# Another order of issue at the seams of a two-layer hybrid decoder trunk in float32 on one core

## The chip, the cores and the metric

The kernel runs on one core of a Trainium2 chip. The metric is the device time of one execution in microseconds, as the median of several runs; the profile is of one execution, whose own time stands below. Engines are named as the trace does: PE is TensorE's matmul, PEld its weight load, DVE VectorE, ACT ScalarE, POOL GpSimd, SP SyncE. Each engine works through its own queue in the order in which the program issues its instructions, and waits at the first one whose operands or buffers are not ready.

## The reference

Two layers work on x of shape 1 x 512 x 1024 in float32. Each layer is this:

```python
h  = rmsnorm(x, ln_mix_g)
qa, ka, va, qb, kb, vb, cq, ckv, kr = split(h @ w_in)   # 3 x 512, 512, 512, 512, 768, 256, 32
ya = dilated_attention(qa, ka, va)        # 8 heads of 64, T5 bias
yb = diff_attention(qb, kb, vb, lambda)   # 4 heads; lambda from lambda_q1, k1, q2, k2
yc = latent_attention(rmsnorm(cq) @ w_uq, rmsnorm(ckv) @ w_ukv, rope(kr))   # 8 heads
m  = sum over branches of sigmoid(h @ w_gate) * (y @ w_br)
x  = x + m @ w_o
f  = rmsnorm(x, ln_ffn_g)
x  = x + (silu(f @ w_ffn_gate) * (f @ w_ffn_up)) @ w_ffn_down   # hidden 2816
```

After the second layer, the output is rmsnorm(x, final_norm_g).

## The kernel before

**Products.** Every float32 product is made of three matmuls in the faster float32 format: high part by high part, high by low, low by high. Weights arrive through SP's queue as tiles of 128 x 1024, a unit. `_hi` makes the high part with a cast on ACT, `_lo` the low part with a subtraction on DVE. `ahead(i, most)` (L272) loads units as far as the present look (`NEAR`, `FAR`, `LEAN`) allows and issues at most so many casts and splits beyond unit i; `prep(n)` makes the first n units at once. A pool of 36 wide tiles (`w`) holds weights, their parts and most intermediates.

**Jobs.** `t_job` (L295) makes a feature-major tile in one PSUM bank with 24 matmuls. `n_job` (L345) makes token-major products: four token blocks of 128 rows, a bank each, with the weights as moving operand; a unit holds two k-blocks. Its list `groups` says how many k-blocks are done for a token block before the next one has its turn. There are four PSUM banks for jobs (`d`, taken round in a ring) and four for attention (`a`).

**A layer.** The norm and its transposes come first, then the value projection. `weave` (L392) interleaves the attention's threads with the dense jobs (queries and keys, `cq`, `ckv`, the up-projections, gates, branches); it decides by a model of its own of when each engine is free, so its order is fixed when the kernel is built. Then come two `n_job`s of w_o, the FFN, and two `n_job`s of w_ffn_down, each of half the columns. All engines' instructions are recorded at L158, the helper that issues them; places are told apart by tiles.

**The start of layer 0.** `after(tb)` transposes a token block of the normed h and splits it; `prep` stands between these calls. `small_setup` is a thread of the weave that computes lambda (small dots on DVE of loaded lambda vectors) and scales of the gates.

**The FFN.** The first two groups are computed by 16 plain products in `ffn_head`, the rest by seven products per group (`P1` to `P7`, Strassen-like, with sums made before on DVE and results evicted by `evac`). The 2816 hidden columns lie in tiles of 1024 columns (`ff32`), each split into high and low by `ffsplit`. The SiLUs of the head's results come after its last product:

```python
o = K.wide(F32)
nc.scalar.activation(o[:, :512], d["X"], AF.Silu)
nc.scalar.activation(o[:, 512:], d["Y"], AF.Silu)
```

**The end.** `final_evac` (L1326 and on) adds the residual, sums squares on ACT, and after the second half calls `norm_block`, which scales both halves on DVE, with the norm's weight, and sends them out through SP.

Of the kernel before, what the change touches and what calls it, by code (L numbers as in the profile page):

```python
# [18 lines left out]
P = 128  # L19
# [148 lines left out]
class Kernel:  # L168
# [176 lines left out]
    def n_job(self, wname, layer, ks, cols, lhs, evac, groups=None, ready=None):  # L345

        w = len(cols)
        per = 1024 // w
        assert per == 2 or len(ks) % 2 == 0
        per = 2  # L350
        units = [[(wname, layer, k, cols) for k in ks[i:i + per]] for i in range(0, len(ks), per)]
        groups = groups or [1] * len(ks)

        def body(j):
            ps = None
            k0 = 0
            for g in groups:
                for tb in range(NT):
                    if g > 1 or tb == 0:
                        self.ahead(j.base + (k0 + g - 1) // per, 2)  # L360
                    if k0 == 0:
                        if ps is None:
                            ps = [None] * NT
                        ps[tb] = self.bank()
                    for kb in range(k0, k0 + g):
                        u, c = j.base + kb // per, slice(kb % per * w, kb % per * w + w)
                        h, l = self.hi[u][:, c], self.lo[u][:, c]
                        ah, al = lhs(kb, tb)
                        o = ps[tb][:, :w]
                        mm = self.nc.tensor.matmul  # L370
                        mm(o, ah, h, start=kb == 0, stop=False)
                        mm(o, ah, l, start=False, stop=False)
                        mm(o, al, h, start=False, stop=kb == len(ks) - 1)
                        if g > 1 and kb == k0 + g // 2 - 1:
                            yield
                    if k0 + g == len(ks):
                        evac(tb, ps[tb])
                    if g > 1 or tb == 1:
                        yield
                k0 += g  # L380
                for u in range((k0 - g) // per, k0 // per):
                    self.done(j.base + u)
                if g == 1:
                    yield

        return self.add_job(units, body, ready)

# [238 lines left out]
def layer(K, l, plan, state, strip, C):  # L626
# [554 lines left out]
    def ffn_head():  # L1181

        for th in range(2):
            for g in range(HEAD):
                d = G[g]
                if th == 0:
                    d["X"], d["Y"] = K.bank(), K.abank()
                for ch in range(2):
                    for kh in range(2):
                        product(d["YX"[ch]][:, th * 256:th * 256 + 256], "A%d%d" % (th + 1, kh + 1),  # L1190
                                d["B%d%d" % (kh + 1, ch + 1)], kh == 0)
                        yield
        for g in range(HEAD):
            d = G.pop(g)
            if g % 2 == 0:
                o = K.wide(F32)
                nc.scalar.activation(o[:, :512], d["X"], AF.Silu)
                nc.scalar.activation(o[:, 512:], d["Y"], AF.Silu)
                V["fg", g // 2] = o
            else:  # L1200
                f = V.pop(("fg", g // 2))
                sub(f[:, :512], f[:, :512], d["X"], ALU.mult)
                sub(f[:, 512:], f[:, 512:], d["Y"], ALU.mult)
                V["ff32"][g // 2] = f
        del SF["A21"]

    def prep(job, g, st):
# [60 lines left out]
    def ffn_run(job):  # L1268
# [6 lines left out]
        for i, (g, p) in enumerate(slots):  # L1275
# [20 lines left out]
                    before()  # L1296
                before = lambda g=g, p=p: evac(g, p)
            K.load_ahead(job.base + 2 * min(NG, slots[min(len(slots) - 1, i + 12)][0] or 4))
            if g == NG - 1 or i > len(slots) - 12:
                K.ahead(job.base + 2 * NG - 1, 1)  # L1300
                if V["nsplit"] < 3:
                    ffsplit(V["nsplit"])
            yield i
        before()
        SF.clear()
# [21 lines left out]
    def final_evac(hf):  # L1327
        def evac(tb, ps):
            t = state["x"][tb][hf]
            nc.vector.tensor_tensor(t, ps, t, op=ALU.add)  # L1330
            if hf == 0:
                state["ss"][tb] = K.small(2)
            K.sumsq(t, state["ss"][tb][:, hf:hf + 1], D)
            if hf == 1:
                xn = K.norm_block(state["x"][tb], state["ss"][tb], state["g"])
                for i in range(2):
                    nc.sync.dma_start(ap["out"][tb * P:tb * P + P, i * 512:i * 512 + 512], xn[i])
        return evac


# [75 lines left out]
                nc.sync.dma_start(state["x"][tb][hf], src[tb * P:tb * P + P, hf * 512:hf * 512 + 512])  # L1416

    def small_setup():
        yield when((), lambda: C["small_tiles"])
        C["setup_small"]()  # L1420

    j_wo = [K.n_job("w_o", l, range(KD), rng(0, 512), mblk, residual_evac(0, ffn_after)),
# [2 lines left out]
    last = l == DEPTH - 1  # L1425
    ev = final_evac if last else (lambda hf: residual_evac(hf, after))
    j_dn = [K.n_job("w_ffn_down", l, range(NF), rng(0, 512), ffblk, ev(0)),
            K.n_job("w_ffn_down", l, range(NF), rng(512, 512), ffblk, ev(1), groups=[1] * 14 + [8])]


    def drain(jobs):
# [3 lines left out]
    def run():  # L1435
        if l == 0:
# [2 lines left out]
            bias = C["setup_bias"]()  # L1439
            next(bias)  # L1440
            norm1_stats(0)
            after(0)
            next(bias)
            K.prep(1)
            norm1_stats(1)
            K.prep(3)
            norm1_stats(2)
            K.prep(4)
            next(va)
            after(1)  # L1450
            norm1_stats(3)
# [48 lines left out]
        K.look = LEAN  # L1500
        drain(j_dn[:1])
        for i, _ in enumerate(K.dense(j_dn[1:])):
            if i == 26:
                K.look = FAR

    plan.append(run)
# [35 lines left out]
```

## Time and profile before

| | us |
|---|---|
| median of 3 runs (1862.61 to 1864.9) | 1864.62 |
| the profiled execution | 1862.47 |
| its span | 1860.7 |
| PE busy in it (98%) | 1818.6 |
| DVE busy (60%) | 1111.1 |
| ACT busy (47%) | 880.3 |

The mean granted clock over the span is 0.998 of TensorE's full speed. Busy time of an engine counts from an instruction's start to its end; matmuls overlap, so one row's mean duration is longer than the distance between two starts.

### The profile page before, as it was taken

How to read it: one execution, taken by the hardware profiler on the slowest of the kernel's cores; microseconds unless marked ns; L12 is line 12 of the kernel's file. 1: busy time of each engine (PE TensorE's matmuls, PEld its weight loads, DVE VectorE, ACT ScalarE, POOL GpSimd, SP SyncE). 2: the span in 40 equal slices, each digit the busy share in tenths (PEclk: the TensorE clock that was granted, in tenths of full speed). 3: DMA queues.
4: the chain of work that ended last, by engine and by line, in shares of the span. 5: the costliest groups of instructions: out<-in, count | busy, mean ns of one | idle time of the engine just before them, and what ended most of it. 6: DMA issues, size and time to landing. Idle time of an engine off the chain costs nothing.

```text
span 1860.7 us, 27128 instructions
## 1 busy us (share of the span) xinstructions
PE 1818.6 (98%) x10588; PEld 1620.2 (87%) x10588; DVE 1111.1 (60%) x1828; ACT 880.3 (47%) x1697; POOL 251.0 (13%) x437
## 2 busy tenths in 40 slices
PE   7999999999999999999999999999999999999998
PEld 5899888888889999988889998888888889999886
DVE  4556555556455888872355565555663578788531
ACT  4456555554334545452235655555443345545430
POOL 3323422212000000000003243122110000000000
PEclk9999999999999999999999999999999999999999
DMA  7332123223340332342433221232242313233331
GB/s 267 108 96 72 52 69 97 85 80 115 124 146 23 99 106 92 113 137 69 147 121 102 69 65 47 72 102 85 69 176 79 114 54 106 91 114 103 125 102 46
DMA packets 63279, 183.14 MB, mean 98 GB/s; under 512 B 9296, under 2 KB 10768, under 8 KB 63152
## 3 DMA queue, kind: packets, MB, share of 16 engines
q1 hardware_dynamic: 58032, 173.89, 28.3%
q0 software_dynamic: 3824, 4.91, 0.9%
q10 hardware_dynamic: 1296, 2.62, 0.4%
q8 instruction: 83, 1.36, 0.3%
q14 instruction: 44, 0.36, 0.1%
HBM read 177.15 MB, written 8.16 MB: 100 GB/s over the span
## 4 chain that ended last, share of the span: by engine, by line
PE 87%; ACT 4%; DVE 4%; issue 2%; POOL 2%; DMA 1%; POOLq 0%; DVEq 0%; ACTq 0%
PE d L158 68%; PE a L158 19%; DVE w L158 3%; ACT w L158 3%; POOL s L158 1%; POOL w L158 1%; DMA w<-in_lambda_k 0%; ACT s L158 0%; DMA s<-in_c_onehot 0%; DVE s L158 0%; ACT junk L158 0%; ACT L158 0%; POOL m L158 0%; DVE f_A L158 0%; DVE f_S L158 0%
## 5 line engine op out<-in xcount | busy, mean ns | idle before, releaser
L158 PE MATMUL d<-w,w 128*128 128x512 f32 (+2 forms) x3888 | 749.4, 347 | 12.2 <-DVE w L158 6.7
L158 PEld LDWEIGHTS d<-w,w 128*128 128x128 f32 x3888 | 631.2, 190 | 96.2 <-ACT s L158 7.2
L158 DVE TENSOR_TENSOR w<-w,w 128x1024 fp32r<-128x1024 f32 (+6 forms) x594 | 597.9, 1031 | 194.8 <-ACT w L158 167.5
L158 PE MATMUL d<-h,w 128*128 128x512 f32 x1920 | 462.1, 393 | 2.8 <-DVE w L158 2.8
L158 ACT CAST w<-w 128x1024 fp32r<-128x1024 f32 (+3 forms) x454 | 399.8, 921 | 101.9 <-DVE w L158 51.7
L158 PEld LDWEIGHTS d<-h,w 128*128 128x128 f32 x1920 | 356.8, 188 | 74.5 <-DVE w L158 3.2
L158 PE MATMUL d<-w,h 128*128 128x512 f32 (+2 forms) x960 | 197.9, 355 | 11.2 <-DVE w L158 9.6
L158 PEld LDWEIGHTS d<-w,h 128*128 128x128 f32 x960 | 164.6, 189 | 30.7 <-issue 9.4
L158 ACT ACTIVATE w<-w,m 128x128 f32<-128x128 f32 x192 | 107.0, 558 | 120.8 <-DVE m L158 119.1
L158 POOL TENSOR_SCALAR m<-m 128x1 f32<-128x1 f32 (+1 forms) x44 | 15.9, 360 | 1085.9 <-ACT junk L158 1085.4
L158 PE MATMUL a<-w,w 128*128 128x256 f32 (+7 forms) x912 | 158.3, 311 | 0.0
L158 PEld LDWEIGHTS a<-w,w 128*128 128x128 f32 (+1 forms) x912 | 138.8, 190 | 11.8
L158 PE MATMUL a<-f_A,w 128*128 128x256 f32 x1104 | 147.9, 285 | 0.0
L158 PEld LDWEIGHTS a<-f_A,w 128*128 128x128 f32 x1104 | 139.6, 193 | 0.0
L158 POOL TENSOR_SCALAR w<-w,m 128x128 f32<-128x128 f32 (+3 forms) x160 | 92.6, 597 | 328.0 <-DVE m L158 219.3
L158 DVE TENSOR_TENSOR w<-a,w 128x512 fp32r<-128x512 f32 (+2 forms) x162 | 90.8, 594 | 75.7 <-ACT w L158 75.4
L158 ACT CAST w<-a 128x512 fp32r<-128x512 f32 (+2 forms) x146 | 70.9, 535 | 68.6 <-PE a L158 67.6
L158 ACT ACTIVATE junk<-s 128x512 f32<-128x512 f32 (+1 forms) x40 | 23.6, 590 | 161.4 <-DVE s L158 161.0
L158 ACT COPY s<-d 128x256 f32<-128x256 f32 (+2 forms) x104 | 39.8, 391 | 108.0 <-PE d L158 107.3
L158 POOL TENSOR_SCALAR w<-w 64x512 fp32r<-64x512 f32 (+1 forms) x96 | 69.4, 730 | 137.3 <-issue 90.1
L158 DVE TENSOR_TENSOR s<-d,s 128x512 f32<-128x512 f32 x32 | 21.9, 689 | 107.6 <-PE d L158 107.6
L158 PE MATMUL a<-ident,w 128*128 128x128 f32 x616 | 83.9, 275 | 0.1
(76 smaller groups left out, 1213.6 us busy)
## 6 DMA issues: line engine op xcount, KB each, us to landing
w<-in_weights SPq DMA_DIRECT2D x246, 512.0 KB, 3.6
w<-in_weights SPq DMA_DIRECT2D x50, 256.0 KB, 2.6
w<-in_weights SPq DMA_DIRECT2D x28, 384.0 KB, 4.4
s<-u_rep SPq DMA_DIRECT2D x24, 256.0 KB, 4.0
w<-in_weights SPq DMA_DIRECT2D x8, 288.0 KB, 2.9
w<-in_x SPq DMA_DIRECT2D x8, 256.0 KB, 7.2
s<-in_x SPq DMA_DIRECT2D x8, 256.0 KB, 5.9
x_dram<-s ACTq DMA_DIRECT2D x8, 256.0 KB, 3.6
```

Source lines behind the costliest of these rows:

```text
L158: return f(*args, **kw)
```

## The change

It puts the same computation in another order in six places. (1) `n_job` does both k-blocks of a unit, six matmuls, for a token block before it goes on to the next, where it did three; `ahead` is called for each token block, with one cast and one split, where it was called once with two; the second down job's list changes in the same way, with its look switched one yield later. (2) In `ffn_head`, the SiLU of each half is issued as soon as the half is complete, and the two products of DVE behind the head. (3) `ffn_run` spreads the three `ffsplit`s and calls of `ahead` over the last eight products, where it had called them from twelve products before the end. (4) `final_evac` multiplies by the norm's weight before the scale is known, scales one half on DVE and the other on ACT, and sends the halves out from two queues. (5) `small_setup` waits until the second `ckvT` tile is there. (6) The first unit is prepared before the first token block's transposes and splits, and the others are one apart. Layer 1 has no part in (5) and (6).

```diff
--- before.py
+++ after.py
@@ -349,15 +349,14 @@
         assert per == 2 or len(ks) % 2 == 0
         per = 2
         units = [[(wname, layer, k, cols) for k in ks[i:i + per]] for i in range(0, len(ks), per)]
-        groups = groups or [1] * len(ks)
+        groups = groups or [2] * (len(ks) // 2)
 
         def body(j):
             ps = None
             k0 = 0
             for g in groups:
                 for tb in range(NT):
-                    if g > 1 or tb == 0:
-                        self.ahead(j.base + (k0 + g - 1) // per, 2)
+                    self.ahead(j.base + (k0 + g - 1) // per, 2 if g > 2 else 1)
                     if k0 == 0:
                         if ps is None:
                             ps = [None] * NT
@@ -371,17 +370,14 @@
                         mm(o, ah, h, start=kb == 0, stop=False)
                         mm(o, ah, l, start=False, stop=False)
                         mm(o, al, h, start=False, stop=kb == len(ks) - 1)
-                        if g > 1 and kb == k0 + g // 2 - 1:
+                        if g > 2 and kb == k0 + g // 2 - 1:
                             yield
                     if k0 + g == len(ks):
                         evac(tb, ps[tb])
-                    if g > 1 or tb == 1:
-                        yield
+                    yield
                 k0 += g
                 for u in range((k0 - g) // per, k0 // per):
                     self.done(j.base + u)
-                if g == 1:
-                    yield
 
         return self.add_job(units, body, ready)
 
@@ -1189,19 +1185,20 @@
                     for kh in range(2):
                         product(d["YX"[ch]][:, th * 256:th * 256 + 256], "A%d%d" % (th + 1, kh + 1),
                                 d["B%d%d" % (kh + 1, ch + 1)], kh == 0)
+                        if th == 1 and g % 2 and kh == 1:
+                            u, n = G[g - 1]["YX"[ch]], 512 - 512 * ch
+                            if ch == 0:
+                                f = K.wide(F32)
+                            nc.scalar.activation(f[:, n:n + 512], u, AF.Silu)
+                            if ch == 1:
+                                V["ff32"][g // 2] = f
                         yield
+        for g in range(1, HEAD, 2):
+            f = V["ff32"][g // 2]
+            sub(f[:, 512:], f[:, 512:], G[g]["Y"], ALU.mult)
+            sub(f[:, :512], f[:, :512], G[g]["X"], ALU.mult)
         for g in range(HEAD):
-            d = G.pop(g)
-            if g % 2 == 0:
-                o = K.wide(F32)
-                nc.scalar.activation(o[:, :512], d["X"], AF.Silu)
-                nc.scalar.activation(o[:, 512:], d["Y"], AF.Silu)
-                V["fg", g // 2] = o
-            else:
-                f = V.pop(("fg", g // 2))
-                sub(f[:, :512], f[:, :512], d["X"], ALU.mult)
-                sub(f[:, 512:], f[:, 512:], d["Y"], ALU.mult)
-                V["ff32"][g // 2] = f
+            del G[g]
         del SF["A21"]
 
     def prep(job, g, st):
@@ -1296,10 +1293,11 @@
                     before()
                 before = lambda g=g, p=p: evac(g, p)
             K.load_ahead(job.base + 2 * min(NG, slots[min(len(slots) - 1, i + 12)][0] or 4))
-            if g == NG - 1 or i > len(slots) - 12:
+            rest = len(slots) - i
+            if rest in (8, 5, 3, 1):
+                ffsplit(V["nsplit"])
+            if rest in (6, 4, 2):
                 K.ahead(job.base + 2 * NG - 1, 1)
-                if V["nsplit"] < 3:
-                    ffsplit(V["nsplit"])
             yield i
         before()
         SF.clear()
@@ -1331,10 +1329,14 @@
             if hf == 0:
                 state["ss"][tb] = K.small(2)
             K.sumsq(t, state["ss"][tb][:, hf:hf + 1], D)
+            sub(t, t, state["g"][hf], ALU.mult)
             if hf == 1:
-                xn = K.norm_block(state["x"][tb], state["ss"][tb], state["g"])
-                for i in range(2):
-                    nc.sync.dma_start(ap["out"][tb * P:tb * P + P, i * 512:i * 512 + 512], xn[i])
+                r = K.rstd([state["ss"][tb][:, 0:1], state["ss"][tb][:, 1:2]])
+                x = state["x"][tb]
+                nc.vector.tensor_scalar(x[0], x[0], r, None, op0=ALU.mult)
+                nc.scalar.activation(x[1], x[1], AF.Copy, scale=r)
+                for i, eng in enumerate((nc.sync, nc.scalar)):
+                    eng.dma_start(ap["out"][tb * P:tb * P + P, i * 512:i * 512 + 512], x[i])
         return evac
 
 
@@ -1416,7 +1418,7 @@
                 nc.sync.dma_start(state["x"][tb][hf], src[tb * P:tb * P + P, hf * 512:hf * 512 + 512])
 
     def small_setup():
-        yield when((), lambda: C["small_tiles"])
+        yield when((("ckvT", 1),), lambda: C["small_tiles"])
         C["setup_small"]()
 
     j_wo = [K.n_job("w_o", l, range(KD), rng(0, 512), mblk, residual_evac(0, ffn_after)),
@@ -1425,7 +1427,7 @@
     last = l == DEPTH - 1
     ev = final_evac if last else (lambda hf: residual_evac(hf, after))
     j_dn = [K.n_job("w_ffn_down", l, range(NF), rng(0, 512), ffblk, ev(0)),
-            K.n_job("w_ffn_down", l, range(NF), rng(512, 512), ffblk, ev(1), groups=[1] * 14 + [8])]
+            K.n_job("w_ffn_down", l, range(NF), rng(512, 512), ffblk, ev(1), groups=[2] * 7 + [8])]
 
 
     def drain(jobs):
@@ -1439,13 +1441,13 @@
             bias = C["setup_bias"]()
             next(bias)
             norm1_stats(0)
+            K.prep(1)
             after(0)
             next(bias)
-            K.prep(1)
+            K.prep(2)
             norm1_stats(1)
-            K.prep(3)
+            K.prep(4)
             norm1_stats(2)
-            K.prep(4)
             next(va)
             after(1)
             norm1_stats(3)
@@ -1500,7 +1502,7 @@
         K.look = LEAN
         drain(j_dn[:1])
         for i, _ in enumerate(K.dense(j_dn[1:])):
-            if i == 26:
+            if i == 27:
                 K.look = FAR
 
     plan.append(run)
```

The names in the rows below are tiles with their numbers, output, an arrow, inputs. On PE, layer 0, at the beginning of the `cq` job (`d` are its four banks, `w_506` and `w_512` the high and low part of its first unit before, `h_0_0` and `h_0_1` high and low part of h for the token block; each piece reads on in the same way):

```order
L158 MATMUL d_627<-w_506,h_0_0_143 128x384
L158 MATMUL d_627<-w_512,h_0_0_143 128x384
L158 MATMUL d_627<-w_506,h_0_1_144 128x384
L158 MATMUL d_631<-w_506,h_0_0_143 128x384
L158 MATMUL d_631<-w_512,h_0_0_143 128x384
L158 MATMUL d_631<-w_506,h_0_1_144 128x384
```

```order
L158 MATMUL d_605<-w_492,h_0_0_147 128x384
L158 MATMUL d_605<-w_498,h_0_0_147 128x384
L158 MATMUL d_605<-w_492,h_0_1_148 128x384
L158 MATMUL d_605<-w_492,h_0_0_147 128x384
L158 MATMUL d_605<-w_498,h_0_0_147 128x384
L158 MATMUL d_605<-w_492,h_0_1_148 128x384
L158 MATMUL d_612<-w_492,h_0_0_147 128x384
```

The second block of rows is that of the change: the first bank gets six matmuls before the second is touched, and so the fourth bank is reached at the 19th matmul and not at the tenth.

On ACT, layer 0, around the end of the FFN's head, first before and then in the change (`d_5461` and `a_5462` are X and Y of the gate's group, `s_5727` or `s_5730` the copy of the first Strassen product):

```order
L158 CAST w_5646<-w_5263 128x512
L158 CAST w_5690<-w_5676 128x1024
L158 CAST w_5706<-w_5263 128x1024
L158 CAST w_5722<-w_5265 128x1024
L158 ACT_TABLE_LOAD
L158 ACTIVATE w_5742<-d_5461 128x512
L158 ACTIVATE w_5742<-a_5462 128x512
L158 CAST w_5760<-w_5475 128x512
L158 COPY s_5727<-d_5725 128x256
```

```order
L158 CAST w_5646<-w_5263 128x512
L158 ACT_TABLE_LOAD
L158 ACTIVATE w_5690<-a_5462 128x512
L158 CAST w_5692<-w_5676 128x1024
L158 CAST w_5708<-w_5263 128x1024
L158 ACTIVATE w_5690<-d_5461 128x512
L158 CAST w_5725<-w_5265 128x1024
L158 CAST w_5760<-w_5475 128x512
L158 COPY s_5730<-d_5728 128x256
```

The table load and the SiLU of Y moved ahead of three casts of 1024 columns, the SiLU of X ahead of one.

On DVE, layer 0, at the last group of the FFN, first before and then in the change (the row that reads a `d` and an `s` tile is the eviction of the fifth product; `w_7942`, `w_7966`, `w_7989` are splits by `ffsplit` before, `w_7963` the split of the down-projection's first unit; in the change `w_7986` and `w_8042` are splits by `ffsplit`):

```order
L158 TENSOR_TENSOR w_7932<-w_7900,w_7898 128x1024
L158 TENSOR_TENSOR w_7942<-w_5742,w_7941 128x1024
L158 TENSOR_TENSOR w_7898<-w_7900,w_7932 128x512
L158 TENSOR_TENSOR w_7963<-w_7935,w_7961 128x1024
L158 TENSOR_TENSOR w_7966<-w_5824,w_7965 128x1024
L158 TENSOR_TENSOR w_7984<-d_7866,s_7869 128x256
L158 TENSOR_TENSOR w_7989<-w_6062,w_7988 128x1024
```

```order
L158 TENSOR_TENSOR w_7932<-w_7900,w_7898 128x1024
L158 TENSOR_TENSOR w_7898<-w_7900,w_7932 128x512
L158 TENSOR_TENSOR w_7966<-d_7866,s_7869 128x256
L158 TENSOR_TENSOR w_7948<-w_7932,w_7947 128x1024
L158 TENSOR_TENSOR w_7966<-a_7867,s_7868 128x512
L158 TENSOR_TENSOR w_7986<-w_5690,w_7985 128x1024
L158 TENSOR_TENSOR w_7964<-w_7898,w_7963 128x1024
L158 TENSOR_TENSOR w_7982<-w_7900,w_7981 128x1024
L158 TENSOR_TENSOR w_8042<-w_5824,w_8041 128x1024
```

The three splits that stood ahead of the eviction stand behind it.

The lambda rows of DVE (eight `ISA` rows and six small ones) stood between the key tile's subtractions and the split of the next unit; in the change that split follows the subtractions directly.

## Rows read from the trace of the kernel before

**Rows 1.** The page's list of engines: busy time, share of the span, instructions.

```profile
PE 1818.6 (98%) x10588; PEld 1620.2 (87%) x10588; DVE 1111.1 (60%) x1828; ACT 880.3 (47%) x1697; POOL 251.0 (13%) x437
```

**Rows 2.** Waits of PE, whole span: total us, times, longest us.

```profile
PE d L158 <- DVE w L158: 19.0, 16, 2.8
```

**Rows 3.** A long piece of the chain: start, us, engine and tile, instructions.

```profile
1731.99 121.16 PE d L158 x540
```

**Rows 4.** Windows: length; PE, PEld, DVE, ACT, POOL busy; clock; DMA; GB/s.

```profile
62.00:67.00 5.00, 4.24 (x14) 3.54 (x15) 4.89 (x7) 2.14 (x4) 0.00 (x0) 0.66 0.03 9
615.00:620.00 5.00, 4.62 (x26) 4.62 (x27) 4.72 (x6) 1.78 (x5) 0.00 (x0) 0.66 0.39 116
1531.00:1536.00 5.00, 4.38 (x36) 4.38 (x37) 4.90 (x7) 1.78 (x5) 0.00 (x0) 1.00 0.44 152
```

**Rows 5.** Timeline at the start: start us, us, instruction, idle before and releaser.

```profile
12.11 0.69 DVE L158 TENSOR_TENSOR h<-a,h 128x512 fp32r<-128x512 f32 x1 [1.85 <-ACT h L158]
...
13.93 0.79 PE L158 MATMUL d<-w,h 128*128 128x512 f32 x1 [1.62 <-ACT w L158]
...
24.48 1.28 DVE L158 TENSOR_TENSOR h<-a,h 128x512 fp32r<-128x512 f32 x2
```

**Rows 6.** Timeline around the lambda set-up.

```profile
58.98 0.23 DVE L158 CUSTOM_DVE_ANT_0 junk<-w 128x64 f32<-128x64 f32 x1 [1.31 <-DMA w<-in_lambda_k]
...
61.48 2.09 DVE L158 TENSOR_TENSOR w<-w,w 128x1024 fp32r<-128x1024 f32 x2
...
62.76 1.85 PE L158 MATMUL d<-h,w 128*128 128x512 f32 x4 [2.76 <-DVE w L158]
...
64.40 1.06 PE L158 MATMUL a<-w,w 128*128 128x128 f32 x4
```

**Rows 7.** Timeline at two job starts, and PE's waits from 66 to 600 us.

```profile
70.99 1.75 PE L158 MATMUL d<-w,h 128*128 128x384 f32 x9
...
72.41 1.41 DVE L158 TENSOR_TENSOR w<-d,w 64x512 fp32r<-64x512 f32 x2 [2.34 <-ACT w L158]
...
73.97 0.76 PE L158 MATMUL d<-w,h 128*128 128x384 f32 x3 [1.22 <-DVE w L158]
...
129.95 1.34 PE L158 MATMUL d<-w,h 128*128 128x288 f32 x9
...
132.92 1.29 PE L158 MATMUL d<-w,h 128*128 128x288 f32 x8 [1.63 <-DVE w L158]
...
PE d L158 <- DVE w L158: 5.4, 5, 1.6
```

**Rows 8.** Timeline at the first Strassen product of layer 0.

```profile
609.20 2.95 ACT L158 CAST w<-w 128x1024 fp32r<-128x1024 f32 x3 [4.54 <-DVE w L158]
...
612.17 1.28 ACT L158 ACT_TABLE_LOAD   x1
...
615.38 2.44 PE L158 MATMUL d<-w,w 128*128 128x256 f32 x12 [2.36 <-ACT s L158]
```

**Rows 9.** Timeline at the last group of the FFN, layer 0.

```profile
801.39 4.26 DVE L158 TENSOR_TENSOR w<-w,w 128x1024 fp32r<-128x1024 f32 x4 [0.26 <-ACT w L158]
...
805.57 0.42 DVE L158 TENSOR_TENSOR w<-d,s 128x256 f32<-128x256 f32 x1
806.04 1.70 PE L158 MATMUL d<-w,w 128*128 128x256 f32 x12 [1.72 <-DVE w L158]
...
811.23 0.98 PE L158 MATMUL d<-w,w 128*128 128x256 f32 x6 [0.28 <-ACT s L158]
```

**Rows 10.** Timeline behind the last matmul.

```profile
1853.18 0.69 DVE L158 TENSOR_TENSOR s<-d,s 128x512 f32<-128x512 f32 x1 [1.44 <-PE d L158]
1853.96 0.63 ACT L158 ACTIVATE junk<-s 128x512 f32<-128x512 f32 x1 [4.71 <-DVE s L158]
...
1855.76 1.41 DVE L158 SCALAR_TENSOR_TENSOR w<-s,m,w 128x512 f32<-128x512 f32 x2 [1.89 <-POOL m L158]
```

**Rows 11.** The page's DMA issues: count, KB each, median us to landing.

```profile
w<-in_weights SPq DMA_DIRECT2D x246, 512.0 KB, 3.6
```

## The prediction

> **What bounds the kernel now.** I began with the page's list of engines [rows 1]: TensorE is busy 98% of the span, DVE 60%. A change that only reorders can win no more than the time in which TensorE stands still or runs at half clock, and its other side is a wait on TensorE that it makes. The waits of TensorE came next [rows 2]: 19.0 us on DVE's writes of wide tiles, 16 times, the largest sum; the row below it is the start-up. Between waits the matmuls follow each other without a hole: a piece of the chain of 540 matmuls of 512 columns takes 121.16 us, 224 ns each [rows 3]; so the order of matmuls in a full stretch is worth nothing, and what counts are the places where TensorE starts late. The windows show what a wait costs behind it [rows 4]: after the 2.76 us wait near 62 us the mean granted clock of 5 us is 0.66, part of it at 1.2 GHz instead of 2.4; near 615 us the same, but at 1531 us, behind the same 2.36 us wait of layer 1, it is 1.00. The timeline then gives each place, below.
>
> All sums stand against the profiled execution, 1862.47 us (span 1860.7 and 1.8 around it); the median of the runs, 1864.62, lies 2.15 above it, and I carry the sum over to the median.
>
> **First split ahead of the transposes (layer 0 only).** DVE idles 1.85 us before 12.11, waiting for ACT's cast of the transposed h; then it does two h splits, a bias product, and only then the first weight's split; TensorE's first projection starts at 13.93 after 1.62 us of waiting for ACT's cast of that weight [rows 5]. With the weight ahead, its split of some 1.2 us (three of this size and a sum of half of it take 4.26 us in [rows 9]) fits into the 1.85, and the first matmul can start up to 1.62 us earlier. But the second token block's h split, at 24.48 with no wait ahead of it [rows 5], has all the splits and norms before it but that one; DVE sets the pace there, and what is left of the gain is the one split moved into idle time. I take -1.1; ends 0 and -1.6.
>
> **Lambda's set-up later (layer 0 only).** Eight small dots and updates stand in DVE's queue between the key eviction and a weight split; one waits 1.31 us for the load of lambda_k, and the split behind them starts only at 61.48 [rows 6]. TensorE waits 2.76 us for it, to 62.76. The order rows show the split directly behind the eviction, so it starts about 4.5 us earlier and is done before TensorE wants it at 60.0: the 2.76 goes, and so does the half clock behind it: 4 matmuls take 1.64 us (62.76 to 64.40, [rows 6]) where 4 x 0.224 is 0.90, so 0.74, and the 4 short ones of that row some 0.4 more. From start to start the hole itself is 2.9, so -4.1 together. At the new place, at the beginning of the second query up-projection, the loads have landed for over 100 us; what stands in DVE's queue there is the 4.7 us from the eviction's end (56.8) to 61.48 without its waits, some 2.4, and the matmuls of that job read nothing that is split behind it in time to matter: 0. Ends -2.8 (only the hole) and -4.5.
>
> **Token-major products by weight tile.** A token-major job needs four PSUM banks. The fourth is still held by the key tile of the job before: its casts and its two DVE subtractions end some 2.8 us after the tile's last matmul. In the old order the fourth bank is wanted at the tenth matmul: 9 of 384 columns from 70.99, and the tenth at 73.97, 1.22 us late by the waits, released by DVE's subtractions from 72.41 [rows 7]. In the new order the fourth bank is wanted at the 19th: nine more matmuls, 9 x 174 = 1.57 us at 384 columns (from 70.99's row, less its drain), 9 x 0.224 = 2.0 at 512, 9 x 133 = 1.20 at 288. Each layer has five such waits, 5.4 us from 66 to 600 us and the largest 1.6, at the 288-column job [rows 7]; from start to start each costs some 0.17 more (70.99 + 9 x 0.174 = 72.56; to 73.97 it is 1.41), 6.2 in all. All are covered but the 288-column one, of which some 0.5 stays. So -5.5 for a layer, -11 for both; ends -8 (0.8 of each wait comes back, because the third bank or the second left operand comes late) and -12.5. Casts and splits of the next tiles go out one at a token block instead of two at the first: the same number of instructions, no more work. Attention pieces shift by a few microseconds in TensorE's order, some transposes of the low-rank query stand closer to their evictions; I count +1 a layer for new short waits, +2, with 0 and +4 as ends (the longest present wait of that stretch is 1.6).
>
> The Trainium skill, "TensorE: Matmul & The Clock Gate", section "A second HAM failure mode: psum-queue depth-cycling", says that going round PSUM banks makes TensorE idle briefly between groups and lose throughput; by it, half as many changes of bank would win something beyond the waits, which no row prices. The trace disagrees: in the last down-projections, which change bank every three matmuls in their first parts, they follow at 224 ns each with no hole [rows 3]. I give it nothing.
>
> **SiLU in the head of the FFN.** After the head products ACT has three casts queued, loads a table for 1.28 us, does two SiLUs and a cast, and only then copies the first Strassen product out of its bank; TensorE waits 2.36 us for that copy, to 615.38 [rows 8]. Yet ACT was idle 4.54 us before 609.20 [rows 8]. The order rows put the table load and the first SiLU ahead of the casts, in that idle time. What stays before the copy is one SiLU and casts; the second SiLU waits for X, which is complete only shortly before the end of the head. Table load and one SiLU, 1.28 + 0.5, leave the queue: the wait falls by 1.8 in each layer, to about 0.6. In layer 0 the half clock goes too: 26 matmuls in 4.62 us, where layer 1 does 36 in 4.38, 122 ns each [rows 4]; 26 x 0.122 = 3.16, so 1.46. Sum -1.8 - 1.8 - 1.5 = -5.1; ends -3.5 (no clock) and -7.
>
> Half clock is in this sum twice, 1.2 and 1.5 us. The Trainium skill, the same page, Part 1, says that the half-rate state is the default, that activity releases it, and that this varies from run to run. The trace agrees at least that equal waits had 0.66 and 1.00 [rows 4]. By the rule neither can be counted on, and the sum would be 2.7 us smaller, which lies inside my range.
>
> **Splits of the FFN's result, spread.** Three splits and a short sum stand in DVE's queue from 801.39 to 805.6, ahead of the eviction of the fifth product (805.57); TensorE waits 1.72 us for it, and 0.28 us again at 811.23 for ACT's copies [rows 9]. The order rows show the eviction directly behind the prep of the last group, with the three splits of 1.2 us behind it one by one. From start to start the waits there cost 1.88 + 0.24 + 0.44 = 2.5 a layer (806.04, 809.49, 811.23). The splits are then done some microseconds before the down-projection reads them. -5.1 for both layers; ends -4 and -5.7.
>
> **End of the kernel.** After the last matmul DVE adds 0.69 us, ACT squares 0.63, GpSimd makes the scale, and two DVE products of about 0.7 each follow from 1855.76, then two output transfers issued by one queue [rows 10]. With the weight factor multiplied in before the scale is known and the two halves scaled on DVE and ACT side by side, one product of 0.7 leaves the path: -0.75; ends -0.4 and -1. The new mult, however, waits for ACT's square sum in the first half of the last down-projection: add 0.69, square 0.63, its read 0.2, mult 0.69 and hops are some 2.3 us a token block on DVE's queue, where a token block's end comes every six matmuls, 6 x 0.224 = 1.34 us. Four of them push the splits of the next job's second tile to about 0.9 us behind need: +0.9; ends 0 and +1.5.
>
> Sum: -1.1 - 4.1 - 11 - 5.1 - 5.1 - 0.75 + 0.9 + 2 = -24.3. That is 1838.2 for the profiled execution and **1840** for the median. All terms at their good ends give -32.3 (1.6 + 4.5 + 12.5 + 7 + 5.7 + 1), at their bad ends -13.2 (2.8 + 8 + 3.5 + 4 + 0.4 - 1.5 - 4): 1832 and 1851.
>
> **Rivals.** *The waits at job starts only move.* In the new order the left operand of the second k-block is wanted at the fourth matmul instead of the thirteenth, and a late split of a weight tile is met sooner. If one of these is what comes last at the five starts, the 11 us stay lost: -13.3, **1851**. For it: DVE has most of its load there. Against it: DVE's subtractions from the bank are what ended the waits shown [rows 7], and the left operands are those of jobs before. *A slower kernel by buffers.* The lambda inputs keep one of the 36 wide tiles for some 125 us longer, while more tiles are wanted at once; weight loads are then issued late, and TensorE waits for landings of 3.6 us [rows 11]. It takes 24.3 / 3.6, seven such late loads, to eat the sum, and eight or more for a slower kernel; with nine, 1840 + 32 = **1872**. Against it: no row of TensorE's waits names a weight load [rows 2]. *No change:* what is won ahead of the weave is lost in it, since the weave interleaves by its own model: within 3.7 us of **1865**.
>
> **Numbers.** 0.72 for the forecast, 0.18 for moved waits, 0.05 slower by buffers, 0.05 no change. 0.2%, 3.7 us, is about what a measurement of this kernel can tell from no change. The range is that of the terms with the moved waits at its upper end: 1831 to 1852. Faster 0.91, same 0.05, slower 0.04, the small rest of the slower case being within the bound.
>
> **What would show it.** In the changed kernel: first projection at about 12.4 us; no wait of TensorE near 60 us and a granted clock near 1.00 in 60 to 65; at job starts no wait before the 19th matmul but at the 288-column job; a wait under 0.8 us at the first Strassen product; none over 0.3 us at the last group; one short DVE wait early in the last job; 7 us instead of 7.6 from the last matmul's end to the span's. The prediction is wrong if TensorE's waits on DVE's wide tiles stay above 10 us.

## The result and the profile after

The changed kernel takes 1838.49 us (median of 4 runs, 1837.4 to 1839.35); the kernel before, run beside it, 1863.61 us (4 runs, 1862.6 to 1864.9). The ratio is 0.9865 with a 95% interval of 0.9847 to 0.9882: 25.1 us less. The prediction was 1840 and 24.3 us less. The profiled execution, 1839.35 us with a span of 1837.6, is 23.1 us below that of before.

TensorE's waits in the changed kernel, whole span (total us, times, longest us), answer to [rows 2]:

```profile
PE a L158 <- DMA s<-in_c_onehot: 7.9, 1, 7.9
PE a L158 <- DVE s L158: 2.3, 2, 2.0
PE d L158 <- DVE w L158: 2.0, 5, 0.5
PE d L158 <- DVE h L158: 1.8, 1, 1.8
PE d L158 <- ACT s L158: 0.9, 2, 0.4
PE a L158 <- DVE w L158: 0.3, 1, 0.3
```

The 19.0 us on DVE's wide tiles are 2.0 now. Two rows are new: 2.3 us on DVE's half-size tiles (`s`) and 1.8 us on its splits of h.

Where it was won is read best by the start of the same matmul (same number in TensorE's order, at places where both orders agree again) in both traces. Each line's gain is the change of the difference since the line above; the prediction's terms stand beside it.

| stretch that ends there | before, us | after, us | difference | gain | predicted |
|---|---|---|---|---|---|
| start of layer 0 (matmul 60) | 28.09 | 28.29 | +0.20 | +0.2 | -1.1 |
| lambda (220) | 67.20 | 62.77 | -4.43 | -4.6 | -4.1 |
| weave and w_o, layer 0 (2750) | 557.50 | 547.52 | -9.98 | -5.6 | -5.5 + 1 |
| FFN head, layer 0 (3130) | 618.89 | 605.75 | -13.15 | -3.2 | -1.8 - 1.5 |
| FFN end, layer 0 (4760) | 817.56 | 801.43 | -16.13 | -3.0 | -2.55 |
| weave, layer 1, first part (6200) | 1102.34 | 1081.66 | -20.68 | -4.6 | |
| weave and w_o, layer 1, rest (8000) | 1464.23 | 1445.19 | -19.04 | +1.6 | -5.5 + 1 with the line above |
| FFN head, layer 1 (8420) | 1533.63 | 1512.70 | -20.93 | -1.9 | -1.8 |
| FFN end, layer 1 (10010) | 1727.27 | 1703.50 | -23.77 | -2.8 | -2.55 |
| both last jobs (10587, the last) | 1852.75 | 1829.78 | -22.97 | +0.8 | +0.9 |
| end of the span | 1860.7 | 1837.6 | -23.1 | -0.1 | -0.75 |

At the places of [rows 6 to 8] the timeline of the changed kernel now has these rows:

```profile
58.23 2.88 PE L158 MATMUL d<-h,w 128*128 128x512 f32 x12
...
66.31 4.69 PE L158 MATMUL d<-w,h 128*128 128x384 f32 x24
...
594.70 1.28 ACT L158 ACT_TABLE_LOAD   x1
...
599.22 2.00 ACT L158 CAST w<-w 128x1024 fp32r<-128x1024 f32 x2 [2.63 <-DVE w L158]
...
603.49 1.70 PE L158 MATMUL d<-w,w 128*128 128x256 f32 x12 [0.45 <-ACT s L158]
```

And these are windows of it (columns as in [rows 4]) where the two holes of layer 0 were, and behind a wait in layer 1 told of below:

```profile
60.00:65.00 5.00, 5.00 (x26) 4.23 (x26) 3.91 (x9) 2.17 (x5) 0.00 (x0) 1.00 0.28 80
603.40:608.40 5.00, 4.91 (x41) 4.92 (x42) 4.90 (x7) 1.41 (x4) 0.00 (x0) 1.00 0.42 136
...
1099.20:1104.20 5.00, 4.98 (x16) 3.99 (x17) 4.54 (x9) 2.50 (x7) 4.83 (x7) 0.66 0.02 5
```

TensorE runs through 60 us without a wait; the `cq` job's first 24 matmuls are one group, 4.69 us, without the wait after nine; the table load lies more than 8 us ahead of the first Strassen product, whose wait is 0.45 us instead of 2.36. The first two windows are at full clock, 2.4 GHz. The FFN's end has these rows.

```profile
789.62 0.42 DVE L158 TENSOR_TENSOR w<-d,s 128x256 f32<-128x256 f32 x1 [1.14 <-PE d L158]
...
791.71 3.50 DVE L158 TENSOR_TENSOR w<-w,w 128x1024 fp32r<-128x1024 f32 x3
...
790.78 1.60 PE L158 MATMUL d<-w,w 128*128 128x256 f32 x12
```

The eviction of the fifth product (789.62) stands ahead of a group of three splits (791.71), of which by the order rows the first is that of the FFN's result, and the product that waited 1.72 us in [rows 9] starts at 790.78 without a wait.

What was not foreseen at its size: at the start the first projection does begin 2.01 us earlier (11.92; 0.21 of it because the very first matmul starts earlier, at 7.91 instead of 8.12), but at 23.87 TensorE waits 1.81 us for the second token block's split of h, behind a weight split of the next job, and the clock falls behind that wait (e5 has the window); and in layer 1 a wait of 2.03 us stands near 1099 us, with GpSimd busy and ACT and DVE waiting for it, and the clock down to a mean of 0.66 behind it, the last window above. The timeline rows:

```profile
22.00 1.22 DVE L158 TENSOR_TENSOR w<-w,w 128x1024 fp32r<-128x1024 f32 x1
...
23.13 1.28 DVE L158 TENSOR_TENSOR h<-a,h 128x512 fp32r<-128x512 f32 x2
...
23.87 2.36 PE L158 MATMUL d<-w,h 128*128 128x512 f32 x6 [1.81 <-DVE h L158]
...
1090.93 2.99 POOL L158 TENSOR_SCALAR w<-w,m 128x128 f32<-128x128 f32 x4 [5.70 <-DVE m L158]
...
1096.97 0.58 ACT L158 COPY s<-a 64x512 f32<-64x512 f32 x1 [3.21 <-POOL s L158]
...
1098.48 0.68 DVE L158 TENSOR_TENSOR s<-a,s 64x512 f32<-64x512 f32 x1 [6.48 <-POOL s L158]
...
1099.22 0.44 PE L158 MATMUL a<-ident,w 128*128 128x128 f32 x2 [2.03 <-DVE s L158]
```

### The profile page after: what moved, and what is told of

It reads as the page before. It is cut to its first block, busy times and chain, and to the rows that moved or that the text cites. A ratio compares the mean times of both kernels' runs of the same rounds, so it can differ in the third digit from the quotient of the medians.

```text
span 1837.6 us, 27149 instructions
## 1 busy us (share of the span) xinstructions
PE 1814.9 (99%) x10588; PEld 1619.2 (88%) x10588; DVE 1112.1 (61%) x1832; ACT 883.1 (48%) x1701; POOL 251.0 (14%) x437
## 3 DMA queue, kind: packets, MB, share of 16 engines
HBM read 177.15 MB, written 8.16 MB: 101 GB/s over the span
## 4 chain that ended last, share of the span: by engine, by line
PE 94%; DVE 2%; ACT 2%; POOL 1%; issue 0%; DMA 0%; POOLq 0%; ACTq 0%
PE d L158 74%; PE a L158 21%; DVE w L158 1%; ACT w L158 1%; POOL s L158 1%; DVE s L158 0%; ACT junk L158 0%; DMA s<-in_c_onehot 0%; POOL w L158 0%; POOL m L158 0%; DVE f_A L158 0%; DVE f_S L158 0%; ACT f_A L158 0%; ACT s L158 0%; DVE h L158 0%
```

## The experiments

Times are medians of runs on the same chip as runs of the kernel before; e1 to e4 stand beside 1863.24 us of it, e5, e7, e8 and e10 beside 1862.79, e6, e11, e12 and e13 beside 1863.59. Differences of less than about 2 us between two of these medians are not told apart by them; there the place in the trace decides.

### One part alone, or one part undone

**e1: the token-major order alone** (in the kernel before).

```diff
-        groups = groups or [1] * len(ks)
+        groups = groups or [2] * (len(ks) // 2)
...
-                    if g > 1 or tb == 0:
-                        self.ahead(j.base + (k0 + g - 1) // per, 2)
+                    self.ahead(j.base + (k0 + g - 1) // per, 2 if g > 2 else 1)
```

> The kernel before with the token-major order by weight tile alone. Theory (each part removes its own holes, and the parts add): the five job-start waits of each layer go but for about 0.5 us at the 288-column job; in layer 1 a new wait of some 2 us of TensorE on DVE, behind GpSimd's rotations, near the query up-projection comes with this part, as in the changed kernel; 8.5 us less than before, about 1855, and the lambda hole of 2.8 us and the FFN waits of 2.4 and 1.7 us stay. Rival (the new wait of layer 1 comes from another part, which shifts the woven order): 11 us less, about 1852.5, and no wait over 1 us in layer 1 between 1080 and 1250 us.

1853.39 us, ratio 0.9948 (0.9934 to 0.9963): 9.9 less. The two rows are TensorE's two waits that the theories are about:

```profile
62.70 1.63 PE L158 MATMUL d<-h,w 128*128 128x512 f32 x4 [2.40 <-DVE w L158]
...
1108.99 0.44 PE L158 MATMUL a<-ident,w 128*128 128x128 f32 x2 [2.07 <-DVE s L158]
```

The new wait of layer 1 comes with this part, and at that place the rival falls, though the time lies between the two forecasts, nearer the rival's. The lambda hole, 2.76 us in [rows 6], is 2.40 here.

**e2: the token-major order undone** (in the changed kernel, the reverse of that diff).

> The changed kernel with the token-major order of before. Theory (the parts add): the ten job-start waits are back, the new wait in layer 1 is gone, about 8.5 us more than the changed kernel, about 1847. Rival (the other parts win part of their time only through the new order): 12 us more or worse, about 1851.

1851.11 us, ratio 0.9938 (0.9921 to 0.9954): 12.6 more than the changed kernel, as the rival has it. The job starts make up the theory's part, but TensorE has two more waits of 1.18 us at the beginning of the last job, where the banks of the last layer's first down-projection are evicted, rows of TensorE first and then of DVE:

```profile
1780.13 0.97 PE L158 MATMUL d<-w,w 128*128 128x512 f32 x3 [1.18 <-DVE s L158]
1782.28 2.07 PE L158 MATMUL d<-w,w 128*128 128x512 f32 x4 [1.18 <-DVE s L158]
...
1778.78 0.69 DVE L158 TENSOR_TENSOR s<-s,w 128x512 f32<-128x512 f32 x1 [0.85 <-ACT junk L158]
1779.39 0.68 DVE L158 TENSOR_TENSOR s<-d,s 128x512 f32<-128x512 f32 x1
```

The new end evicts a bank every 2.15 us, because its mult waits for ACT's square sum; in the old order the next job wants a bank every three matmuls. So the end needs the order: with it the job loses 0.8 us, without it 4.9 (how far the starts of matmuls 10010 and 10360 lie ahead of those of before: 23.77 and 22.97 us in the changed kernel, 16.22 and 11.28 here).

**e3: lambda's set-up undone** (in the changed kernel).

```diff
-        yield when((("ckvT", 1),), lambda: C["small_tiles"])
+        yield when((), lambda: C["small_tiles"])
```

> The changed kernel with lambda's set-up at its early place. Theory: the hole near 60 us is back with 2.8 us and a granted clock of about 0.66 behind it, 4.5 us more than the changed kernel, about 1843. Rival (the small work costs the same where it now stands, only in pieces that the list of waits does not show): less than 2 us more.

1840.19 us, ratio 0.9876 (0.9861 to 0.989): 1.7 more, the rival's size, but not for the rival's reason alone. The hole is back at half its size (timeline), and the window behind it is at full clock:

```profile
58.28 0.22 DVE L158 CUSTOM_DVE_ANT_0 junk<-w 128x64 f32<-128x64 f32 x1 [0.29 <-DMA w<-in_lambda_k]
...
61.81 1.20 PE L158 MATMUL d<-h,w 128*128 128x512 f32 x4 [1.50 <-DVE w L158]
```

```profile
61.80:66.80 5.00, 4.99 (x24) 4.28 (x25) 4.89 (x10) 1.95 (x5) 0.00 (x0) 1.00 0.02 9
```

The load wait that was 1.31 us in [rows 6] is 0.29. From matmul 220 on (2.54 ahead of before, where the changed kernel has 4.43) the run then gets back most of the rest: at the end of layer 0's w_o it is 9.5 ahead and the changed kernel 10.0, since the small waits of the changed order at the `ckv` job and at 196 us are not there.

**e4: the FFN's two parts undone** (SiLUs behind the head, the three splits together).

> The changed kernel with the SiLUs behind the head and the three splits together, as before. Theory: the waits of 2.4 us at the first and of 1.7 us at the last Strassen group are back in both layers, 11 us more than the changed kernel with a spell at the lower clock, 9.5 without, so 1848 to 1849.5. Rival (in the changed kernel the evictions behind the splits pay part of it back): 6 us more or less.

1851.25 us, ratio 0.994 (0.9925 to 0.9955): 12.8 more. TensorE's waits of this run:

```profile
PE d L158 <- DVE w L158: 6.0, 7, 1.7
PE d L158 <- ACT s L158: 5.0, 3, 2.4
```

The waits are back; the granted clock behind the first of them is 0.66 in both layers this time, where in [rows 4] only layer 0 had it, and 0.66 in layer 0 behind the second of them too (795.1 to 800.1 us; 1.00 in the kernel before, 806 to 811). Each such spell costs some 1.5 us, and the theory counted one. The theory holds, its bound was set too low by that.

**e5: the start undone** (`prep(1)` behind the first `after`, then 3 and 4, as before).

> The changed kernel with the first weights prepared in the old places. Theory (the part wins nothing where the second token block's split of h sets the pace): TensorE's waits up to 60 us add up to the same 7.5 to 7.9 us, in other places, and the time is that of the changed kernel within 1 us, about 1838.5. Rival (the prediction's step: the one split moved into idle time stays won): 1.1 us more.

1837.96 us, ratio 0.9869 (0.9855 to 0.9884): the changed kernel's time. Matmul 60 starts at 28.41, in the changed kernel at 28.29. That the part wins nothing is not the whole of it, though. Other runs have the changed start too, and behind the same wait they fall into two kinds; the changed kernel and then e7, the wait's row and the 5 us behind it (columns as in [rows 4]):

```profile
23.87 4.06 PE L158 MATMUL d<-w,h 128*128 128x512 f32 x10 [1.81 <-DVE h L158]
23.87:28.87 5.00, 5.00 (x19) 4.02 (x20) 2.53 (x5) 0.38 (x1) 3.17 (x5) 0.66 0.15 47
```

```profile
23.97 2.57 PE L158 MATMUL d<-w,h 128*128 128x512 f32 x10 [1.76 <-DVE h L158]
23.97:28.97 5.00, 5.00 (x26) 4.25 (x27) 3.82 (x7) 1.07 (x2) 3.15 (x5) 1.00 0.14 40
```

From TensorE's first matmul to matmul 60 it is 19.96 us here and 19.97 in the kernel before; with the changed start it is 18.80 to 18.81 where the clock stays up (e2, e4, e7) and 20.26 to 20.38 where it falls (the changed kernel, e3, e6, e10). So the part wins 1.2 us, as the prediction's step has it, and loses 0.3 to 0.4 where half clock follows the wait that is left.

**e6: the end undone** (`norm_block` as before).

> The changed kernel with the end of before (both halves scaled and weighted on DVE after the scale is known). Theory (as written, the part costs 0.7 us in the last layer's first down-projection, and GpSimd beside the mult takes back most of what the end wins): the wait of 0.42 us in that job goes, the time from the last matmul to the span's end stays at 7.8 to 7.9 us, 0.6 us less than the changed kernel. Rival (the prediction's sum for both: the end wins 0.75): 0.15 us more or less, with the end 0.7 us longer.

1838.92 us, ratio 0.9866 (0.9852 to 0.9879), no difference that the runs tell. In the trace TensorE's wait at the beginning of the last job, behind the first down-projection's evictions, is gone (0.7 us), and from the last matmul's start to the span's end it is 7.63 us against 7.80 (7.63 to 7.64 in e1 and e11 too, but 7.94 in the kernel before; 7.80 to 7.81 in e2, e4, e5 and e8; e3, e10 and e13, with the changed end, have 8.16 to 8.38): the places go with the theory, its 0.6 us is below what the medians resolve.

**e11: lambda's set-up alone** (in the kernel before).

> The kernel before with the late set-up of lambda alone. Theory (the part's worth depends on when the loads of lambda land, and in the start of before they land late): the hole of 2.76 us and the half clock behind it go, 4.1 to 4.6 us at that place; some waits of the weave behind it come in return, as in the changed kernel (0.4 to 1.2 us), so 3 to 4.5 us less than before, 1859 to 1860. Rival (its worth is that of the run with the part undone, below 2 us): 1861.5 to 1863.

1860.06 us, ratio 0.9978 (0.9969 to 0.9987): 3.5 less. TensorE passes 60 us without a wait, 4.3 us ahead at matmul 220; the next job start waits longer than in [rows 7]:

```profile
61.54 1.53 PE L158 MATMUL d<-h,w 128*128 128x512 f32 x6
...
69.86 0.77 PE L158 MATMUL d<-w,h 128*128 128x384 f32 x3 [1.65 <-DVE w L158]
```

So alone the part wins 3.5 us, and as the last part to be added 1.7 or less.

**e13: lambda's set-up and the start undone.** Is it the start's part that made the loads of lambda early enough to shrink the hole?

> The changed kernel with lambda's set-up early and the start of before. Theory (the first weight's split ahead of the transposes lets the loads of lambda be issued and land earlier, which is why the hole was only 1.5 us with the part on lambda undone alone): the hole near 60 us is 2.4 to 2.8 us with a granted clock of 0.66 behind it, 2.5 us more than with lambda's part undone alone, about 1842.5. Rival (the hole was shorter by chance of the transfers): 1.5 us and a granted clock of 1.00, about 1840.

1840.12 us, ratio 0.9874 (0.986 to 0.9887), that of e3.

```profile
58.95 0.23 DVE L158 CUSTOM_DVE_ANT_0 junk<-w 128x64 f32<-128x64 f32 x1 [1.03 <-DMA w<-in_lambda_k]
...
62.22 1.20 PE L158 MATMUL d<-h,w 128*128 128x512 f32 x4 [1.98 <-DVE w L158]
```

The hole is 1.98 us, between the two theories, and the clock stays at 1.00. The load waits vary with the start and from run to run; how much of the 1.26 us between 2.76 and 1.50 is the start's stays open.

### What the new waits come from

**e8: the next job's first split later** (in the changed kernel, around the first half of the value job).

```diff
+            K.look = NEAR[0], 0, 0
             next(va)
             after(1)
+            K.look = NEAR
```

> The changed kernel with the next job's first weight split behind the second token block's splits of h instead of ahead of them. Theory: TensorE's wait of 1.81 us at 23.87 us falls by the 1.2 us of that split to 0.6, and what is won there stays, 1.2 us less. Rival (the norm of the third block or ACT's casts come last there, or the split is missed at the next seam): within 0.4 us of the changed kernel.

1836.92 us, ratio 0.9862 (0.9847 to 0.9876), 1.6 less. The row that had a wait of 1.81 us:

```profile
23.32 2.57 PE L158 MATMUL d<-w,h 128*128 128x512 f32 x10 [0.68 <-DVE h L158]
```

It falls by 1.13, as the theory says: the split of the next job's weight held TensorE there. From the first matmul to matmul 60 it is 17.68 us (17.70 in e12), 1.1 less than the changed start has at full clock and 2.7 less than in the changed kernel; the other 1.6 are the half clock, which does not follow the shorter wait in either run.

**e10: the rotation's intermediate in a wide tile** (in the changed kernel; no engine's order moves).

```diff
-            tmp = K.slot(F32)
+            tmp = K.wide(F32)
```

> The changed kernel with the rotation's intermediate in a wide tile instead of one of the 11 half-size tiles, every engine's order the same. Theory (the new wait of 2.0 us in layer 1 comes from tiles: ACT and DVE wait for half-size tiles that GpSimd's rotations still read): the wait of TensorE near 1099 us goes, and the half clock behind it, 2 to 3.5 us less. Rival (GpSimd's order itself, four scalings ahead of four rotations, sets it): the wait stays at 2 us.

1835.17 us, ratio 0.9853 (0.9838 to 0.9867), 3.3 less. ACT, DVE and TensorE at the same instructions:

```profile
1093.93 0.58 ACT L158 COPY s<-a 64x512 f32<-64x512 f32 x1 [0.75 <-PE a L158]
...
1094.54 0.68 DVE L158 TENSOR_TENSOR s<-a,s 64x512 f32<-64x512 f32 x1 [3.13 <-ACT s L158]
...
1096.44 0.38 PE L158 MATMUL a<-ident,w 128*128 128x128 f32 x2
```

GpSimd does its four scalings and rotations in the same order, and nobody waits for them: the wait was for one of the 11 half-size tiles. From matmul 6200 to 6600 this run gains 0.3 us on before, where the changed kernel loses 3.6.

**e7: the weight multiplied into a tile of its own** (in the changed kernel; the half is scaled from there).

```diff
-            sub(t, t, state["g"][hf], ALU.mult)
+            sub(state["xg", tb][hf], t, state["g"][hf], ALU.mult)
```

> The changed kernel with the norm's weight multiplied into a tile of its own beside ACT's square sum, so that DVE waits for no square sum and nothing of DVE runs beside GpSimd's scale. Theory (DVE's wait for the square sum costs 0.7 us in the first half of the last down-projection, and the mult beside GpSimd's scale 0.5 us at the end): no wait of TensorE in that job, GpSimd's first scale instruction after the last matmul takes 0.3 us again instead of 0.79, 1.3 us less. Rival (the 0.79 us have another cause, and the wait in the job is the adds and splits themselves): nothing changes by more than 0.3 us.

1837.49 us, ratio 0.9868 (0.9851 to 0.9884). The changed kernel's and then this run's DVE mult and GpSimd scale behind the last matmul:

```profile
1831.69 0.69 DVE L158 TENSOR_TENSOR s<-s,w 128x512 f32<-128x512 f32 x1 [0.79 <-ACT junk L158]
1831.75 0.79 POOL L158 TENSOR_SCALAR m<-m 128x1 f32<-128x1 f32 x1 [4.00 <-ACT junk L158]
```

```profile
1827.22 0.69 DVE L158 TENSOR_TENSOR w<-s,w 128x512 f32<-128x512 f32 x1
...
1828.04 0.30 POOL L158 TENSOR_SCALAR m<-m 128x1 f32<-128x1 f32 x1 [4.50 <-ACT junk L158]
```

Both steps of the theory are seen at their places: GpSimd's 0.79 us is 0.30 as soon as the mult no longer runs beside it, the time from the last matmul's start to the end is 7.30 instead of 7.80 (but 7.60 in e12, with the same end, so how much of the 0.5 is the tile's stays open), and the 0.7 us at the beginning of the last job are gone. The 1.0 us of the medians is too little to be told by itself.

**e12: e7, e8 and e10 together.**

> The changed kernel with the three improvements at once: the weight multiplied into a tile of its own, the next job's first split behind the second token block's, the rotation's intermediate in a wide tile. Theory (they act at different places and add: 1.2, 1.1 and 2 to 3.8 us): 4.5 to 6 us less than the changed kernel, 1832.5 to 1834. Rival (wide tiles run short, or one saving is given back at the next seam): less than 3 us.

1831.98 us (5 runs, 1831.78 to 1832.22), ratio 0.983 (0.9816 to 0.9843): 6.5 less than the changed kernel, 31.6 less than before, the fastest of all. TensorE's waits:

```profile
PE d L158 <- DVE w L158: 1.1, 3, 0.5
PE d L158 <- ACT s L158: 0.9, 2, 0.5
PE d L158 <- DVE h L158: 0.7, 1, 0.7
```

The three act at different places and add. The gain is 0.5 us above the theory's upper bound; in this profiled run the clock is at full speed up to the last matmul, where the changed kernel has half clock behind two waits.

## Why the prediction was right, and where its steps were off

The mechanism stands: a kernel at 98% on TensorE gained what its seams had lost. Of its terms, those of lambda's hole, the job starts of layer 0, the FFN's head and end in both layers and the mult in the last layer's first down-projection came within 1.1 us at their places, and most within 0.5. Undoing the parts brought the waits back where they had been (e2, e4). That the total came so near is in part luck: by the table, terms that fell short by some 3.6 us together, the start and layer 1's weave above all, met others that won some 2.5 more than forecast.

*The start was mis-sized: +0.2 instead of -1.1.* The step said that the one split moved into idle time stays won, and it does: 1.2 us where the clock stays up (e5's paragraph). What the step put at nothing was half clock behind the wait that the second token block's split of h leaves; in the changed kernel it costs 1.6 us and takes the gain back. e8 shows that the next job's weight split, which stands ahead of that split, makes 1.1 us of the wait.

*Half clock, as a whole, won nothing.* Both spells in the sum, 1.2 and 1.5 us, are gone, but the changed kernel's profiled execution has two others, behind the new waits at the start and in layer 1, of some 1.6 us each. The prediction's paragraph on them had said that they can't be counted on.

*The weave of layer 1 was mis-sized: -2.9 instead of -4.5.* Its allowance of 1 us for new short waits met one wait of 2.03 us and 1.6 us of half clock behind it (between matmuls 6200 and 6600 the changed kernel loses 3.6 us on before, e5, with the same wait and full clock behind it, 2.0). The step looked at engines' orders, and missed what no order shows: in the new order ACT and DVE come for half-size tiles while GpSimd's rotations hold them. e1 shows the wait with the order alone, and e10 takes it away with a tile.

*The end was mis-sized: -0.1 instead of -0.75.* The mult was put in its place, but it runs beside GpSimd's scale and makes it 0.49 us longer (e7), and by the commonest values of e6's paragraph the end is 0.17 us longer than with the old form; the table's -0.1 is there because the kernel before itself had 7.94.

*Lambda's term was right in its place (-4.6 for -4.1), but the parts don't add.* Alone it wins 3.5 (e11), and undone it costs 1.7 (e3): with the other parts the loads wait less, the clock stays up, and the late set-up has small costs of its own in the weave. The order part too is 9.9 alone and 12.6 undone. The new end leans on it, with 4.1 us (e2); how much of the rest is the clock's is not settled, since e1's profiled run has half clock at five places ahead of the last matmul and that of before at two. The sum of the prediction, which walked through the whole changed kernel place by place, is not the sum of the single parts.

*The rivals.* Moved waits at job starts: only the 288-column job keeps one, 0.42 us in layer 0 and 0.48 in layer 1, as forecast. Late weight loads: no row of TensorE's waits names one, so lambda's longer hold on a wide tile cost nothing to be seen.

## What to carry to other kernels

Where the bounding engine is busy 98%, list its waits, find for each what stands in the releasing engine's queue ahead of the release without being needed yet, and move that; a bank that is wanted nine matmuls later hides an eviction for nothing. Then ask what the moved instructions share with their new neighbours: a pool of tiles or a neighbour engine took back 3.3 us and 0.5 us here, and no order of instructions shows either. Price parts at their places in the whole, since alone and undone the same part was worth 3.5 and 1.7 us. And before a part is called worthless, look at the granted clock behind the waits it leaves: half clock hid the start's 1.2 us here.

## What the runs showed of the hardware

*The clock after a short wait is not settled by the wait.* Behind the wait of 2.03 to 2.07 us in layer 1, in the same piece of the program, the granted clock of the 5 us after it was 0.66 in the changed kernel, e3, e4, e6 and e8, and 1.00 in e1, e5, e7 and e13. Behind waits of 1.50 and 1.98 us it was 1.00 (e3, e13), behind 2.40 and 2.76 us 0.66 (e1, before), and behind 2.36 us it had both values (layer 0 and layer 1 of the kernel before). Behind the start's wait of 1.76 to 1.81 us it was 0.66 in the changed kernel, e3, e6 and e10, and 1.00 in e2, e4 and e7; behind 1.72 us at the FFN's end of layer 0, 1.00 in the kernel before and 0.66 in e4. The Trainium skill, "TensorE: Matmul & The Clock Gate", Part 1, calls the start of full speed run-variable. Of the clock's fall behind a wait these rows show the same. A wait of 2 us is so worth 2 us or 3.6 on this kernel, and two profiles that differ by 1.6 us may differ in nothing else.

*DVE beside GpSimd.* A GpSimd operation on 128 x 1 elements took 0.30 us with DVE idle (e7) and 0.79 us beside a DVE product of 128 x 512 with both operands in SBUF (the changed kernel); that is its own duration, behind its wait for data. All four of them at the end of the changed kernel took 0.79 and ended 0.17 us behind the product. Beside a DVE product that reads one operand from a PSUM bank the same operation took 0.22 us in the same trace (151.0 and 1054.9 us).
